# The first token group's output projection, taken from the trunk to the mixer's end

## The chip, the cores and the metric

One of the eight cores of a Trainium2 chip. The metric is the device time of one execution in microseconds (us); before the change the median of three runs is 3453.26 us (3449.13 to 3471.99). TensorE (PE) does the matmuls, VectorE (DVE) and ScalarE (ACT) elementwise work, GpSimd (POOL) some of it and some transfers; SyncE (SP) issues most transfers. Each engine works its instructions off in order.

## The reference

One step of a two-layer decoder for a prompt of 1024 tokens and 64 sample tokens, all in float32. The first layer, as far as it matters here:

```
o_tok = rwkv7_mix(rms_norm(x))              # 768 columns, 12 heads, a scan over the tokens
o_mem = memory_attention(q_mem, k, v)       # 256 columns, 4 heads over 256 memory tokens
x = x + concat([o_tok, o_mem]) @ W_o[l]     # 1024 x 1024
f = conv_glu(rms_norm(x, norm_ffn[l]), ...) # the feed-forward part
x = x + f
```

The keys and values of the memory are made for both layers from the same memory tokens. The second layer is of the same kind with latent attention in place of the scan; the outputs are both token sets after a last norm, and the states.

## The kernel before, in words

Activations lie transposed: 1024 features in eight blocks (KC = 8) of 128 partitions, tokens along the free dimension. Prompt and sample tokens form one row of 1088 columns, worked in three groups G3 of 364, 364 and 360. A float32 operand is split into a high part (an ACT cast) and a low remainder (a subtraction on DVE, or on POOL inside the mixer), and each product is three matmuls: wh xh, wh xl, wl xh (`gemm_y`, L477 to L479). Weights come in raw tiles `wr` of 128 x 512 (three buffers, filled from SP, L207), are cast to `wh` (L210) and leave the remainder `wl` (L211), four buffers each.

**The mixer** (`mixer_a`) works head pairs in two token halves. Several generators are merged by weights: at each step the one that is least far on, for its weight, emits its next instructions. `last` ends the mixer: the inner part and scan of the last pair (`main`), the pair before it (`side`) and as filler the first layer's memory attention (L2111 to L2241), and then the second layer's memory keys and values (`memory_kv`, L2051 to L2096). TW holds the weights: TW[4] filler steps beside the chain, TW[7] beside the last output step `a_out` (L1019 to L1058). The mixer's outputs go to the DRAM tensor `od`, through `y` (L1056).

**The trunk** (`Step.trunk_tail` for the first layer) loads `od` group by group into `xl` from POOL's queue (L1452), splits it (L1458, L1459), and fills the stream `x` from nine row tiles `xt` of two buffers (L1140) by eight PE transposes (L1152) and two ACT copies (L1154) each. Then it multiplies: column blocks d = 0 to 3 for the three groups, then d = 4 to 7, each followed by the residual add (L1162), a square (L1167, L1170) and a sum of squares on POOL (L1171). The norm of one group runs beside the products of the next.

A scheduler orders each engine's instructions by the program's order and its own estimates; an instruction that waits holds up all behind it on its engine. A transfer issued from SP or POOL waits at its issue until its buffer is free.

Of the kernel before, what the change touches and what calls it, by code (L numbers as in the profile page):

```python
# [9 lines left out]
F32 = mybir.dt.float32  # L10
F32R = mybir.dt.float32r
I32 = mybir.dt.int32
BF16 = mybir.dt.bfloat16
AF = mybir.ActivationFunctionType
ALU = mybir.AluOpType
# [4 lines left out]
NP_ = 1024  # L20
NS = 64
NT = NP_ + NS
KC = 8
# [62 lines left out]
G3 = [(0, 364), (364, 364), (728, 360)]  # L86
# [14 lines left out]
class Step:  # L101
# [168 lines left out]
            s.nc.sync.dma_start(out=xt[h], in_=s.I["x_prompt"][0, 128 * i:128 * i + 128, 512 * h:512 * h + 512])  # L270
        return xt

    def mixer_a(s, od, qmd, kvd):
        nc, tc = s.nc, s.tc
        s.wl_eng = nc.gpsimd
        ap = s.ap_
        s.od, s.qmd = od, qmd
        s.gate = {}
        s.TW = (50, 0, 110, 0, 60, 10, 50, 120)
        s.PW = (15, 20, 0, 40, 15, 0)  # L280

        def ld(name, shape):
# [33 lines left out]
        for nme, cnt in (("mu_r", 6), ("mu_k", 6), ("mu_v", 6), ("mu_la", 1), ("mu_g0", 1), ("mu_g1", 1)):  # L316
            o = s.t(ap, [128, cnt], "o" + nme, 1)
# [23 lines left out]
        def last(fill):  # L341

            u0, u1 = units[-2:]
            h, p = u1
            c = ctx[u1]

            def main():

                s.ended = True
                yield from s.a_inner(p, h, c)  # L350
                c["y"] = s.t(ap, [128, 576], "y", 2)
                for g in s.groups(h)[:2]:
                    yield from s.a_chain(p, h, c, *g, ("ab", "tp"))

            def side():
                yield from chain(u0)
                while "y" not in c:
                    yield
                yield from s.a_chain(p, h, c, 8, 1)

            w = s.TW
            yield from s.mergeg([(main(), w[0], w[1]), (side(), w[2], w[3]), (s.take(fill, w[4]), w[4])])
            yield from s.mergeg([(s.a_out(p, h, c), w[5], w[6]), (fill, w[7])])
# [5 lines left out]
        for i in range(nu):  # L369
            g = []  # L370
# [10 lines left out]
                g.append((mkv, 22))  # L381
            s.merge(g)
        s.mslot = (ap, "xn", 584, 16)
        s.drain(last(s.seq(s.mem_attention(0, qmd, kvd, od, ("mm", "sm", "sm")), s.memory_kv(kvd, 1, ("sm", "mm", "mm")))))

    def rot(s, name):
        l = getattr(s, name)
# [748 lines left out]
    def x_tile(s, i, eng):  # L1136

        xt = s.st([128, 1024], "xt", 2)
        src = s.I["x_prompt"][0, 128 * i:128 * i + 128] if i < 8 else s.I["x_sample"].rearrange("b t d -> (b t) d")
        eng.dma_start(out=xt[:128 if i < 8 else 64], in_=src)  # L1140
        return xt

    def load_x(s, first):

        nc, x = s.nc, s.x
        for i in range(9):
            rows = 128 if i < 8 else 64
            xt = first[i] if i < len(first) else s.x_tile(i, nc.sync)
            for h in range(2):
                q = s.pst("tp")  # L1150
                for k in range(4):
                    nc.tensor.transpose(q[:, k * 128:k * 128 + rows], xt[:rows, 512 * h + 128 * k:512 * h + 128 * k + 128], s.ident[:rows, :rows])  # L1152
                qv = q.rearrange("p (k t) -> p k t", t=128)[:, :, :rows]
                nc.scalar.copy(x[:, 4 * h:4 * h + 4, 128 * i:128 * i + rows], qv)  # L1154
            yield

    def residual(s, d, g, p, acc):
# [268 lines left out]
    def trunk_tail(s, l, od, xd, qmd, xst):  # L1426

        nc, I = s.nc, s.I
        with s.phase(f"f{l}", {"mm": 4, "dn": 2, "tp": 2}):
            s.xp = s.sp  # L1430
            s.ntb, s.LAG = 4, 2
            xdv = xd.rearrange("(k p) t -> p k t", p=128)
            xs = []

            def normed(g, acc):
                xs.append(s.new_xg())
                return s.norm_x(g, acc, ("norm_ffn", 8 * l), xs[-1])

            with s.sub(f"o{l}"):
                os_ = []  # L1440
                first = []
                if l == 0:

                    sh = dict(acc=([128, 364], "acc", 2), nt=([128, 364], "nt", 4), wl=([128, 4, 128], "wl", 8, F32R), wh=([128, 4, 128], "wh", 8, F32R), xt=([128, 1024], "xt", 2))
                    s.lay(*[sh[z] for z in ('wl', 'wh', 'acc', 'nt', 'xt')])
                for c0, n in G3:
                    if c0 == G3[1][0] and l == 0:
                        first = [s.x_tile(i, nc.gpsimd) for i in range(2)]
                    xh, xl = (s.t(s.xp, [128, KC, 364], z, 3, F32R) for z in ("xh", "xl"))
                    m = min(n, NP_ - c0)  # L1450
                    f = xl.bitcast(F32)
                    nc.gpsimd.dma_start(out=f[:, :, :m], in_=od[0].rearrange("(k p) t -> p k t", p=128)[:, :, c0:c0 + m])  # L1452
                    if m < n:
                        nc.gpsimd.dma_start(out=f[:, :, m:n], in_=od[1].rearrange("(k p) t -> p k t", p=128))
                    os_.append((xh, xl, n))
                def parts(xh, xl, n):
                    for k in range(KC):
                        nc.scalar.copy(xh[:, k, :n], xl[:, k, :n].bitcast(F32))  # L1458
                        nc.vector.tensor_tensor(xl[:, k, :n], xl[:, k, :n].bitcast(F32), xh[:, k, :n].bitcast(F32), ALU.subtract)  # L1459
                        yield  # L1460

                xs_ = [(g, [(xh[:, k], xl[:, k]) for k in range(KC)], 0) for g, (xh, xl, n) in zip(G3, os_)]
                with s.tc.manual_schedule(engines={mybir.EngineType.Activation, mybir.EngineType.DVE}):
                    ws = [s.load_w([(I["w_o"][l, :, 0:128], 0, 128)])]
                    s.drain(parts(*os_[0]))
                    ws += [s.load_w([(I["w_o"][l, :, 128 * d:128 * d + 128], 0, 128)], ring=(s.sp, 8)) for d in range(1, 4)]
                if l == 0:
                    s.drain(s.load_x(first))
                acc = {c0: s.st([128, 364], "acc", 2) for c0, n in G3[:2]}
                acc[G3[2][0]] = s.last_acc()  # L1470
                for d0 in (0, 4):
                    if d0:
                        ws = [s.load_w([(I["w_o"][l, :, 128 * d:128 * d + 128], 0, 128)], ring=(s.sp, 8)) for d in range(d0, d0 + 4)]
                    pend = s.emit(s.gemm_t(ws, d0, xs_, acc, normed if d0 else None, () if d0 else [parts(*z) for z in os_[1:]]))
            xl = []

            def stored(g, acc):
                c0, n = g
                nc.sync.dma_start(out=xdv[:, :, c0:c0 + n], in_=s.x[:, :, c0:c0 + n])
                xl.append(s.new_xg())  # L1480
                return s.split_x(g, acc, xl[-1])

            with s.sub(f"n{l}"):
                pend = s.emit(s.ffn(l, xs, pend, stored if l == 0 else s.final, s.first_latent if l == 0 else None))
                if l:
                    s.drain(pend)
            if l == 0:
                s.ntb = 3
                with s.sub("lat"):
                    s.latents(xl, qmd, pend, xst)  # L1490
        if l:
            xst.close()
# [799 lines left out]
    def run(s):  # L2292
        nc, tc = s.nc, s.tc
        s.ps = s.psb = s.sp = None
        dp = s.ctx.enter_context(tc.tile_pool(name="dp", bufs=1, space=bass.MemoryType.DRAM))
        dt = lambda shape, n: s.t(dp, shape, n, 1)
        s.dp, s.wsum = dp, {}
        od = dt([1024, NP_], "odp"), dt([1024, NS], "ods")
        xd, kvd = dt([1024, NT], "xd"), dt([2, 2, 128, 512], "kvd")
        qmd = [dt([256, NT], f"qmd{l}") for l in range(2)]  # L2300
        with s.phase("a", {"mm": 2, "sm": 1, "so": 1, "ab": 1, "tp": 1, "ch": 1, "y": 1}):
            s.a_begin()
            s.consts()
            s.consts_b()
            s.mixer_a(od, qmd[0], kvd)
        s.wl_eng = nc.vector
        s.trunk_tail(0, od, xd, qmd[1], s.stream(0, "right"))
        xst = s.attention(qmd[1], kvd, od, xd)
        Seven(s).trunk_tail(1, od, xd, None, xst)


class Seven(Step):
# [22 lines left out]
    def squares(s, h, acc):  # L2335

        nc = s.nc
        for d in range(KC):
            for c0, a in acc.items():
                xv = s.x[:, d, c0:c0 + QT]  # L2340
                if d == 0:
                    nc.scalar.activation(a, xv, AF.Square)
                else:
                    sq = s.st([128, QT], "nt", s.ntb)
                    nc.scalar.activation(sq, xv, AF.Square)
                    nc.gpsimd.tensor_tensor(a, a, sq, ALU.add)
            yield
# [416 lines left out]
```

## Time and profile before

| | |
|---|---|
| median of three runs | 3453.26 us |
| the profiled execution | 3465.75 us, span 3464.0 us |
| PE busy | 3314.6 us, 96% |
| DVE, ACT, POOL busy | 59%, 43%, 18% |
| mean granted clock of PE | 0.966 |
| DMA | 347 MB, mean 100 GB/s |

Times in the rows are us from the span's start. Busy time is summed over one engine's instructions. A value in brackets behind an instruction is how long its engine stood idle before it, and what ended that. Matmuls overlap, so a matmul's own duration is longer than the distance to the next.

### The profile page before, as it was taken

Reading aid. Unit: us, or ns where it says so; the run is one execution under the profiler, and the core shown is the slowest. Engines: PE = TensorE matmul, PEld = TensorE weight load, DVE = VectorE, ACT = ScalarE, POOL = GpSimd, SP = SyncE. Lnnn points to the kernel's source line nnn. Section 1 sums busy time; section 2 is a strip of 40 time slices with the busy share of each in tenths; the row PEclk is TensorE's granted clock in tenths of the full one; section 3 lists DMA queues with packets and bytes.
Section 4 is the critical chain, followed back from the end, with each engine's and each line's share of the span. In section 5 each row is a group of like instructions: output and inputs, shape, how many; then the busy total and the mean of one; then the engine's idle time right before and its main releaser. Section 6 shows DMA issues by size and latency. Waiting matters only on the chain. (4 is left out here: it accounts for less than half of the span.)

```text
span 3464.0 us, 63205 instructions
## 1 busy us (share of the span) xinstructions
PE 3314.6 (96%) x24362; PEld 2844.6 (82%) x24362; DVE 2060.9 (59%) x4790; ACT 1502.6 (43%) x3355; POOL 633.3 (18%) x982
## 2 busy tenths in 40 slices
PE   6999999999979999999999999899999999999998
PEld 5555677776569999999999888655669999989998
DVE  5776666776535433334345477634446777787776
ACT  5555445544544312212125445433344545454444
POOL 4323123330011000000003100111113211132221
PEclk9998699998889999999999999999999999999999
DMA  4212011113151435425334210454332544544443
GB/s 119 59 32 85 22 39 35 45 46 98 31 169 59 133 93 113 124 82 110 115 78 104 83 47 28 146 173 164 133 94 83 173 138 143 146 133 141 136 139 116
DMA packets 452626, 347.01 MB, mean 100 GB/s; under 512 B 46202, under 2 KB 425870, under 8 KB 446948
## 3 DMA queue, kind: packets, MB, share of 16 engines
q1 hardware_dynamic: 434052, 263.31, 25.7%
q0 software_dynamic: 14368, 75.00, 7.7%
q10 hardware_dynamic: 3904, 4.65, 0.4%
q8 instruction: 191, 3.13, 0.4%
q14 instruction: 111, 0.91, 0.1%
HBM read 317.13 MB, written 71.89 MB: 112 GB/s over the span
## 5 line engine op out<-in xcount | busy, mean ns | idle before, releaser
L477 PE MATMUL pmm<-xh,wh 128*128 128x364 f32 (+3 forms) x1544 | 509.0, 330 | 4.4 <-ACT xh L2662 3.3
L479 PE MATMUL pmm<-xh,wl 128*128 128x364 f32 (+3 forms) x1544 | 503.6, 326 | 0.0
L478 PE MATMUL pmm<-xl,wh 128*128 128x364 f32 (+3 forms) x1544 | 503.3, 326 | 0.2
L210 ACT CAST wh<-wr 128x512 fp32r<-128x512 f32 (+3 forms) x381 | 219.6, 584 | 392.2 <-PE pmm L478 200.3
L2478 PE MATMUL pmm<-xh,uh 128*128 128x272 f32 x1232 | 357.1, 290 | 4.7 <-ACT uh L2434 3.2
L2479 PE MATMUL pmm<-xl,uh 128*128 128x272 f32 x1232 | 355.9, 289 | 1.6 <-DVE xl L1134 1.6
L2480 PE MATMUL pmm<-xh,ul 128*128 128x272 f32 x1232 | 356.8, 290 | 0.0
L477 PE MATMUL pdn<-hh,wh 128*128 128x272 f32 (+2 forms) x1080 | 329.4, 305 | 3.6 <-DVE x L2324 1.9
L479 PE MATMUL pdn<-hh,wl 128*128 128x272 f32 (+2 forms) x1080 | 328.5, 305 | 0.8 <-DVE wl L211 0.8
L478 PE MATMUL pdn<-hl,wh 128*128 128x272 f32 (+2 forms) x1080 | 328.3, 305 | 0.3 <-DVE hl L1134 0.3
L211 DVE TENSOR_TENSOR wl<-wr,wh 128x512 fp32r<-128x512 f32 (+3 forms) x289 | 187.0, 652 | 208.8 <-ACT wh L210 206.7
L477 PEld LDWEIGHTS pmm<-xh,wh 128*128 128x128 f32 (+1 forms) x1544 | 290.9, 188 | 9.1 <-ACT xh L2662 3.7
L2434 ACT CAST uh<-wa 128x512 fp32r<-128x512 f32 x305 | 188.5, 620 | 244.2 <-PE pmm L2479 155.5
L478 PEld LDWEIGHTS pmm<-xl,wh 128*128 128x128 f32 (+1 forms) x1544 | 291.2, 189 | 2.7 <-issue 0.5
L479 PEld LDWEIGHTS pmm<-xh,wl 128*128 128x128 f32 (+1 forms) x1544 | 291.5, 189 | 1.0
L2435 DVE TENSOR_TENSOR ul<-wa,uh 128x512 fp32r<-128x512 f32 x305 | 216.4, 715 | 49.6 <-ACT uh L2434 37.4
L2478 PEld LDWEIGHTS pmm<-xh,uh 128*128 128x128 f32 x1232 | 232.8, 189 | 5.9 <-ACT uh L2434 3.6
L2479 PEld LDWEIGHTS pmm<-xl,uh 128*128 128x128 f32 x1232 | 232.9, 189 | 2.2 <-DVE xl L1134 2.2
L2480 PEld LDWEIGHTS pmm<-xh,ul 128*128 128x128 f32 x1232 | 232.6, 189 | 0.2 <-DVE ul L2435 0.2
L477 PE MATMUL pmm<-xn,wh 128*128 128x292 f32 (+2 forms) x552 | 206.7, 374 | 3.7 <-DVE e L507 3.7
L477 PEld LDWEIGHTS pdn<-hh,wh 128*128 128x128 f32 x1080 | 202.8, 188 | 6.0 <-ACT hh L1133 3.5
L479 PEld LDWEIGHTS pdn<-hh,wl 128*128 128x128 f32 x1080 | 202.6, 188 | 1.8 <-DVE wl L211 1.3
(792 smaller groups left out, 7509.9 us busy)
## 6 DMA issues: line engine op xcount, KB each, us to landing
wa<-in_w_ffn_up SPq DMA_DIRECT2D x131, 256.0 KB
wr<-in_w_ffn_down SPq DMA_DIRECT2D x114, 256.0 KB
wr<-in_w_ffn_up SPq DMA_DIRECT2D x89, 256.0 KB
wr<-in_w_in_a SPq DMA_DIRECT2D x84, 256.0 KB
wr<-in_w_o SPq DMA_DIRECT2D x48, 256.0 KB
wa<-ws1vg SPq DMA_DIRECT2D x44, 256.0 KB
wa<-ws1all SPq DMA_DIRECT2D x44, 256.0 KB
wa<-ws1vgg SPq DMA_DIRECT2D x43, 256.0 KB
```

The lines of the kernel that those rows point to most:

```text
L210: nc.scalar.copy(wh[:, :n, :m], wr[:, :n, :m])
L211: s.wl_eng.tensor_tensor(wl[:, :n, :m], wr[:, :n, :m], wh[:, :n, :m].bitcast(F32), ALU.subtract)
L477: nc.tensor.matmul(ps[:m, :n], wh[:, :m], xh[:, c0:c0 + n], start=(k == 0), stop=False)
L478: nc.tensor.matmul(ps[:m, :n], wh[:, :m], xl[:, c0:c0 + n], start=False, stop=False)
L479: nc.tensor.matmul(ps[:m, :n], wl[:, :m], xh[:, c0:c0 + n], start=False, stop=(k == last))
L2434: nc.scalar.copy(wh, w)
L2435: nc.vector.tensor_tensor(wl, w, wh.bitcast(F32), ALU.subtract)
L2478: nc.tensor.matmul(p, wh, xh[:, k], start=k == 0, stop=False)
L2479: nc.tensor.matmul(p, wh, xl[:, k], start=False, stop=False)
L2480: nc.tensor.matmul(p, wl, xh[:, k], start=False, stop=k == 3)
```

## The change

A new generator `early_out` is put behind the memory keys and values in the filler. It reloads the first 364 prompt columns of `od` (eight pieces, from SP), splits them, and for each of eight column blocks loads w_o and the matching columns of x, multiplies, transposes x on PE, adds both, and writes the block to the DRAM tensor `xd`. The trunk then loads `od` and fills `x` for groups 1 and 2 alone, loads group 0 of `x` from `xd`, and squares it in a generator of its own; the products of group 0 leave the trunk. Two weights of TW change.

```diff
-        s.TW = (50, 0, 110, 0, 60, 10, 50, 120)
+        s.TW = (50, 0, 110, 0, 100, 10, 50, 160)
...
-        s.drain(last(s.seq(s.mem_attention(...), s.memory_kv(kvd, 1, ("sm", "mm", "mm")))))
+        s.drain(last(s.seq(s.mem_attention(...), s.memory_kv(kvd, 1, ("sm", "mm", "mm")), s.early_out(od, xd))))
+
+    def early_out(s, od, xd):
+
+        nc, I = s.nc, s.I
+        n = G3[0][1]
+        xs = []
+        for k in range(KC):
+            xh, xl = (s.t(s.ap_, [128, 584], "xn", 16, F32R)[:, :n] for _ in range(2))
+            nc.sync.dma_start(out=xl.bitcast(F32), in_=od[0][128 * k:128 * k + 128, :n])
+            xs.append((xh, xl))
+        for xh, xl in xs:
+            nc.scalar.copy(xh, xl.bitcast(F32))
+            nc.vector.tensor_tensor(xl, xl.bitcast(F32), xh.bitcast(F32), ALU.subtract)
+            yield
+        for d in range(KC):
+            c = slice(128 * d, 128 * d + 128)
+            xr = s.t(s.wp, [128, 4, 128], "wr", 3)
+            nc.sync.dma_start(out=xr[:, :2], in_=I["x_prompt"][0, 0:256, c].rearrange("(i p) f -> p i f", p=128))
+            nc.sync.dma_start(out=xr[:n - 256, 2], in_=I["x_prompt"][0, 256:n, c])
+            w = s.load_w([(I["w_o"][0, :, c], 0, 128)])
+            p = s.pst("mm")
+            for k in range(KC):
+                (wh, wl), (xh, xl) = w[k], xs[k]
+                nc.tensor.matmul(p[:, :n], wh, xh, start=k == 0, stop=False)
+                nc.tensor.matmul(p[:, :n], wh, xl, start=False, stop=False)
+                nc.tensor.matmul(p[:, :n], wl, xh, start=False, stop=k == KC - 1)
+                yield
+            q = s.pst("sm")
+            for i in range(3):
+                r = min(128, n - 128 * i)
+                nc.tensor.transpose(q[:, 128 * i:128 * i + r], xr[:r, i], s.ident[:r, :r])
+            o = s.t(s.ap_, [128, 588], "ext", s.XB)[:, :n]
+            nc.scalar.copy(o, q[:, :n])
+            nc.vector.tensor_tensor(o, o, p[:, :n], ALU.add)
+            nc.sync.dma_start(out=xd[c, :n], in_=o)
+            yield
...
-        for i in range(9):
-            rows = 128 if i < 8 else 64
-            xt = first[i] if i < len(first) else s.x_tile(i, nc.sync)
+        for i in range(6):
+            xt, rows = first[i] if i < len(first) else s.x_tile(i, nc.sync)
+            c0 = G3[0][1] + 128 * i
...
-                for c0, n in G3:
-                    if c0 == G3[1][0] and l == 0:
+                for c0, n in G3[1:]:
+                    if c0 == G3[2][0]:
                         first = [s.x_tile(i, nc.gpsimd) for i in range(2)]
...
+                g0 = G3[0]
+                nc.gpsimd.dma_start(out=s.x[:, :, :g0[1]], in_=xdv[:, :, :g0[1]])
...
+                def squares():
+                    a = acc[0][:, :g0[1]]
+                    for d in range(KC):
+                        xv = s.x[:, d, :g0[1]]
+                        sq = s.st([128, 364], "nt", s.ntb) if d else a
+                        nc.scalar.activation(sq[:, :g0[1]], xv, AF.Square)
+                        if d:
+                            nc.gpsimd.tensor_tensor(a, a, sq[:, :g0[1]], ALU.add)
+                        yield
+
-                xs_ = [... for g, (xh, xl, n) in zip(G3, os_)]
+                xs_ = [... for g, (xh, xl, n) in zip(G3[1:], os_)]
...
-                    pend = s.emit(s.gemm_t(ws, d0, xs_, acc, normed if d0 else None, () if d0 else [parts(*z) for z in os_[1:]]))
+                    pend = s.emit(s.gemm_t(ws, d0, xs_, acc, normed if d0 else None, [normed(g0, acc)] if d0 else [parts(*os_[1]), squares()]))
```

How the change moves instructions is read from the order of each engine's program; a line number there is that of the kernel it stands in. First PE at the mixer's end, before: the second half of the output step (`pso`), then the memory keys and values, whose tokens are transposed (`psm`) and multiplied (`pmm`, 128x512).

```order
L1051 MATMUL pso_11146<-g1s_5988,wh_10698 128x288
L1048 MATMUL pso_11152<-g0h_5872,wh_10698 128x288
L1049 MATMUL pso_11152<-g0l_5873,wh_10698 128x288
L1050 MATMUL pso_11152<-g0h_5872,wl_10699 128x288
L1051 MATMUL pso_11152<-g1s_5988,wh_10698 128x288
L2068 MATMUL psm_10980<-ident_93,xn_10954 128x128
```

And now (`wr` under `psm` is the column block of x that `early_out` transposes):

```order
L1087 MATMUL pso_11570<-g1s_5988,wh_10881 128x288
L415 MATMUL psm_11316<-ident_93,wr_11273 128x128 x2
L2138 MATMUL pmm_11001<-xn_11008,xn_11003 128x512
L2138 MATMUL pmm_11002<-xn_11008,xn_11003 128x512
L415 MATMUL psm_11316<-ident_93,wr_11273 128x108
L2139 MATMUL pmm_11001<-xn_11009,xn_11003 128x512
L2140 MATMUL pmm_11001<-xn_11008,xn_11003 128x512
L2139 MATMUL pmm_11002<-xn_11009,xn_11003 128x512
L2140 MATMUL pmm_11002<-xn_11008,xn_11003 128x512
L1084 MATMUL pso_11576<-g0h_5872,wh_10881 128x288
```

The token transposes and the first of eight weight chunks now stand ahead of the output step's last part; the early block's 192 matmuls follow behind the eighth chunk.

SP's queue in the early block, now: the reload of `od` (L393) behind the memory result's six writes (L2145 to L2148).

```order
L393 DMA xn_11137<-odp_63 128x364
L2145 DMA kvd_66<-xn_11126 128x512
L2147 DMA out_mem_k_p<-xn_11126 128x256
L2148 DMA out_mem_v_p<-xn_11126 128x256
L2145 DMA kvd_66<-xn_11131 128x512
L2147 DMA out_mem_k_p<-xn_11131 128x256
L2148 DMA out_mem_v_p<-xn_11131 128x256
L393 DMA xn_11140<-odp_63 128x364
```

Before, these writes were followed by a tile of x, and nothing reloaded `od` from SP. Further on in SP's queue, the loads of the last column block (`wr`, from in_x_prompt and in_w_o) and the write of the sixth:

```order
L419 DMA xd_65<-ext_11468 128x364
L403 DMA wr_11520<-in_x_prompt 108x128
L207 DMA wr_11523<-in_w_o 128x4x128
L207 DMA wr_11529<-in_w_o 128x4x128
```

The loads of column block 8 stand directly behind the write of column block 6.

POOL at the border between mixer and trunk, before (`xl` is the operand of a group, `xt` a tile of x):

```order
L405 TENSOR_TENSOR rstd_10974<-ms_10971,mhalf_91 128x2
L1452 DMA xl_11181<-odp_63 128x8x364
L1140 DMA xt_11183<-in_x_prompt 128x1024
L1140 DMA xt_11185<-in_x_prompt 128x1024
L1452 DMA xl_11188<-odp_63 128x8x364
```

And now:

```order
L211 TENSOR_TENSOR wl_11526<-wr_11523,wh_11525 128x512
L211 TENSOR_TENSOR wl_11532<-wr_11529,wh_11531 128x512
L1492 DMA xl_11605<-odp_63 128x8x364
L1177 DMA xt_11607<-in_x_prompt 128x1024
L1177 DMA xt_11609<-in_x_prompt 128x1024
L1492 DMA xl_11612<-odp_63 128x8x296
L1494 DMA xl_11612<-ods_64 128x8x64
L1497 DMA x_11589<-xd_65 128x8x364
```

The first load of the trunk stood behind the memory tokens' norm; it now stands behind the last weight remainder of the early block.

## Rows read from the trace of the kernel before

**Rows 1.** The core's span and clock, and from the profile's page the busy time and the busy tenths of PE and its granted clock in 40 slices.

```profile
core 0: 3464.0 us, clock 0.966
PE 3314.6 (96%) x24362; PEld 2844.6 (82%) x24362; DVE 2060.9 (59%) x4790; ACT 1502.6 (43%) x3355; POOL 633.3 (18%) x982
PE   6999999999979999999999999899999999999998
PEclk9998699998889999999999999999999999999999
```

**Rows 2.** Stretches around the mixer's end: length, then busy us (and instructions) of PE, its weight loads, DVE, ACT and POOL, PE's granted clock, the share of the DMA engines, GB/s.

```profile
922.20:946.50 24.30, 23.26 (x227) 15.27 (x226) 15.05 (x56) 13.47 (x50) 0.00 (x0) 1.00 0.12 29
946.50:960.20 13.70, 7.79 (x45) 4.77 (x42) 4.46 (x13) 9.55 (x20) 0.00 (x0) 0.89 0.32 98
960.20:986.20 26.00, 19.58 (x64) 13.69 (x64) 11.40 (x23) 10.95 (x23) 3.66 (x5) 0.66 0.56 191
...
986.00:992.00 6.00, 4.14 (x25) 3.33 (x23) 4.68 (x10) 6.00 (x15) 2.23 (x3) 1.00 0.80 251
992.00:1001.00 9.00, 1.64 (x11) 1.30 (x12) 0.79 (x2) 1.66 (x4) 0.00 (x0) 0.85 1.05 378
1001.00:1020.00 19.00, 18.56 (x115) 17.37 (x116) 11.71 (x22) 16.05 (x36) 1.33 (x1) 0.89 0.66 202
...
1036.00:1100.00 64.00, 64.00 (x386) 63.53 (x385) 25.67 (x43) 25.62 (x44) 15.01 (x15) 1.00 0.24 73
```

**Rows 3.** PE's timeline from the output step to the first memory product: start, duration of the piece, instruction, count, idle time before it and what ended it.

```profile
958.76 0.61 PE L1048 MATMUL pso<-g0h,wh 128*128 128x288 f32 x1 [3.85 <-DVE y L1052]
...
962.41 0.45 PE L2068 MATMUL psm<-ident,xn 128*128 128x128 f32 x1 [2.33 <-DVE xn L408]
...
965.02 1.12 PE L2068 MATMUL psm<-ident,xn 128*128 128x128 f32 x4 [0.68 <-ACT xn L2070]
...
971.32 0.79 PE L2086 MATMUL pmm<-xn,xn 128*128 128x512 f32 x1 [1.59 <-ACT xn L1133]
```

**Rows 4.** The memory keys and values: SP's weight loads, a late cast, and two products that follow each other.

```profile
961.50 19.09 SPq L2081 DMA_DIRECT2D xn<-in_w_mem_kv  x8
...
978.00 0.39 PE L2088 MATMUL pmm<-xn,xn 128*128 128x512 f32 x1
...
978.23 0.39 PE L2087 MATMUL pmm<-xn,xn 128*128 128x512 f32 x1
...
981.51 0.62 ACT L1133 CAST xn<-xn 128x512 fp32r<-128x512 f32 x1 [2.11 <-DMA xn<-in_w_mem_kv]
```

**Rows 5.** PE's waits from 800 to 1030 us, by who was waited for: total, times, longest.

```profile
PE ptp L1152 <- DMA xt<-in_x_prompt: 7.2, 1, 7.2
PE pso L1048 <- DVE y L1052: 4.7, 2, 3.8
...
PE pmm L477 <- ACT xh L1458: 1.1, 1, 1.1
```

**Rows 6.** The first and last of SP's six writes of the memory result, and ACT's eight casts of group 0's operand.

```profile
986.43 0.33 SPq L2093 DMA_DIRECT2D kvd<-xn  x1
...
989.35 0.43 SPq L2096 DMA_DIRECT2D out_mem_v_p<-xn  x1
...
986.78 3.28 ACT L1458 CAST xh<-xl 128x364 fp32r<-128x364 f32 x8
```

**Rows 7.** One weight tile of w_o: its issue on SP, the cast that waited for it, and the weight remainders on POOL over the whole run (min/median/max ns).

```profile
1054.00 0.37 SPq L207 DMA_DIRECT2D wr<-in_w_o  x1
...
1056.56 0.62 ACT L210 CAST wh<-wr 128x512 fp32r<-128x512 f32 x1 [3.31 <-DMA wr<-in_w_o]
...
L211 POOL TENSOR_TENSOR wl<-wr,wh x92: 450/1283/1989, 23.7 to 773.1; 128x512 fp32r<-128x512 f32 x88, 128x128 fp32r<-128x128 f32 x4
```

**Rows 8.** POOL's loads of the three groups' operands: when issued, and the time to landing over them.

```profile
961.70 1.08 POOL L1452 DMA_DIRECT2D xl<-odp  x1
...
985.56 1.79 POOL L1452 DMA_DIRECT2D xl<-odp  x2 [21.52 <-DVE xn L1134]
...
DMA to landing us min/median/max: 8.4/10.1/11.9
```

**Rows 9.** The third tile of x: its issue, PE's transposes that waited for it, matmuls behind that wait, matmuls some us later, and eight transposes without a wait.

```profile
989.95 0.36 SPq L1140 DMA_DIRECT2D xt<-in_x_prompt  x1
...
1001.01 1.94 PE L1152 MATMUL ptp<-ident,xt 128*128 128x128 f32 x8 [7.22 <-DMA xt<-in_x_prompt]
...
1003.66 0.51 PE L477 MATMUL pmm<-xh,wh 128*128 128x364 f32 x1
1003.96 0.51 PE L478 MATMUL pmm<-xl,wh 128*128 128x364 f32 x1
...
1005.14 0.33 PE L479 MATMUL pmm<-xh,wl 128*128 128x364 f32 x1
1005.30 0.33 PE L477 MATMUL pmm<-xh,wh 128*128 128x364 f32 x1
...
1006.97 1.04 PE L1152 MATMUL ptp<-ident,xt 128*128 128x128 f32 x8
```

More of the change, by code (lines that the diff above doesn't have):

```diff
@@ L271, in a_load, with mixer_a @@
         return xt
-    def mixer_a(s, od, qmd, kvd):
+    def mixer_a(s, od, qmd, kvd, xd):
         nc, tc = s.nc, s.tc
@@ L383, in mixer_a @@
         s.mslot = (ap, "xn", 584, 16)
-        s.drain(last(s.seq(s.mem_attention(0, qmd, kvd, od, ("mm", "sm", "sm")), s.memory_kv(kvd, 1, ("sm", "mm", "mm")))))
+        s.drain(last(s.seq(s.mem_attention(0, qmd, kvd, od, ("mm", "sm", "sm")), s.memory_kv(kvd, 1, ("sm", "mm", "mm")), s.early_out(od, xd))))
+    def early_out(s, od, xd):
[32 more added lines that the diff above has]
+            yield
     def rot(s, name):
@@ L1138, in x_tile @@
         xt = s.st([128, 1024], "xt", 2)
-        src = s.I["x_prompt"][0, 128 * i:128 * i + 128] if i < 8 else s.I["x_sample"].rearrange("b t d -> (b t) d")
-        eng.dma_start(out=xt[:128 if i < 8 else 64], in_=src)
-        return xt
+        c0 = G3[0][1] + 128 * i
+        n = min(128, NP_ - c0)
+        eng.dma_start(out=xt[:n], in_=s.I["x_prompt"][0, c0:c0 + n])
+        if n < 128:
+            eng.dma_start(out=xt[n:n + NS], in_=s.I["x_sample"].rearrange("b t d -> (b t) d"))
+            n += NS
+        return xt, n
     def load_x(s, first):
         nc, x = s.nc, s.x
-        for i in range(9):
-            rows = 128 if i < 8 else 64
-            xt = first[i] if i < len(first) else s.x_tile(i, nc.sync)
+        for i in range(6):
+            xt, rows = first[i] if i < len(first) else s.x_tile(i, nc.sync)
+            c0 = G3[0][1] + 128 * i
             for h in range(2):
@@ L1153, in load_x @@
                 qv = q.rearrange("p (k t) -> p k t", t=128)[:, :, :rows]
-                nc.scalar.copy(x[:, 4 * h:4 * h + 4, 128 * i:128 * i + rows], qv)
+                nc.scalar.copy(x[:, 4 * h:4 * h + 4, c0:c0 + rows], qv)
             yield
@@ L1460, in parts @@
                         yield
-                xs_ = [(g, [(xh[:, k], xl[:, k]) for k in range(KC)], 0) for g, (xh, xl, n) in zip(G3, os_)]
+                def squares():
[7 more added lines that the diff above has]
+                        yield
+                xs_ = [(g, [(xh[:, k], xl[:, k]) for k in range(KC)], 0) for g, (xh, xl, n) in zip(G3[1:], os_)]
                 with s.tc.manual_schedule(engines={mybir.EngineType.Activation, mybir.EngineType.DVE}):
@@ L1466, in trunk_tail @@
                     ws += [s.load_w([(I["w_o"][l, :, 128 * d:128 * d + 128], 0, 128)], ring=(s.sp, 8)) for d in range(1, 4)]
-                if l == 0:
-                    s.drain(s.load_x(first))
+                s.drain(s.load_x(first))
                 acc = {c0: s.st([128, 364], "acc", 2) for c0, n in G3[:2]}
@@ L2304, in run @@
             s.consts_b()
-            s.mixer_a(od, qmd[0], kvd)
+            s.mixer_a(od, qmd[0], kvd, xd)
         s.wl_eng = nc.vector
```

## The prediction

> **What bounds the kernel now.** I read the profile's page first: TensorE (PE) is busy 96% of the 3464.0 us span, and the busy tenths show where the rest is: the first slice, and the twelfth (about 953 to 1039 us), with 7 tenths [rows 1]. The kernel is bound by PE, so an edit is worth something only where PE stands still or runs at its lower clock. The change touches only the end of the mixer and the first output projection; from the feed-forward part on, PE's order is the same in both kernels. So the second view is the table by stretches around that place [rows 2]. From 946.5 to 960.2 us, the last head pair's output step, PE works 7.79 of 13.7 us. From 960.2 to 986.2, the second layer's memory keys and values, it works 19.58 of 26.0, at a mean clock of 0.66. From 986 to 1020, group 0 of the projection with the fill of the stream, it works 24.3 of 34. Behind that it is full: 386 matmuls in 64.0 us, 0.166 each. So some 22 us of standing still are to be had (5.9 + 6.4 + 9.7), and a few more of low clock.
>
> The third view, PE's timeline and waits, says what ends each pause. The output step waits 3.85 us for a vector step. The transposes of the memory tokens go back and forth with ScalarE from 962.4, and the first product stands at 971.32 [rows 3]. The products then wait for weights: SP needs 19.09 us for eight loads, a cast waits 2.11 us for one, though two products stand 0.23 us apart when nothing is late [rows 4]. At the fill, the longest wait is 7.2 us for the third tile of x; the first operand of the projection costs only 1.1 us, as its load ran under the memory products [rows 5].
>
> **The change part by part** (+ is slower; the profiled execution is the base).
>
> *The moved product.* 192 matmuls (8 column blocks of 8 x 3) of 364 columns leave the trunk, 192 x 0.166 = 31.8 us, and come in at the mixer's end at the same price: 0. The order shows where: not in the waits of the last chain, but in one block behind the last product of the memory keys and values. No pause of the mixer is filled by it.
>
> *Transposes of x.* 72 before (nine tiles of eight), 48 + 24 now. Eight take 1.04 us [rows 9], 0.13 each. Nine of the 24 now stand among the waits of the output step: -1.2.
>
> *The memory keys and values.* More of the attention is drawn into the chain (the table's 60 becomes 100), so this work starts inside the chain and the output step. The front, 960.2 to 971.3, goes off the path: -11.1. What hides it is the 5.9 us in which PE stood in the output step; if ScalarE, which is busy there, holds it up, half of it stays: bound -6. The products took 971.3 to 986.2, 14.9 us. The first of eight weight chunks is now used before the output step ends, the second is loaded by then; the third is queued on SP behind the write of the output step, and the last ones wait for free tiles. Six loads at 2.6 us landing, two by two, put the end about 13 us after that write: -2. Bounds: -5 (42 products at 0.23 make 9.7 us), 0.
>
> *The reload of the operand.* Before, POOL issued it at 961.70, under the memory products. Now seven of the eight pieces stand on SP behind the six writes of the memory result. Those run from 986.43 to 989.78, 3.35 us; the nearest landing is a weight tile, issued at 1054.00 and cast at 1056.56, 2.56 us; a cast is 3.28 / 8 = 0.41 [rows 6, 7]. PE does the first piece (0.5 us) and waits 3.4 + 2.6 + 0.4 - 0.5 = 5.9 us, less the 1.1 that stood there: +5 (bounds 0 to +9).
>
> *Weights for the early block.* It reads all of w_o once more: 16 loads, 16 casts of 0.62 us, 16 remainders on POOL of 1.28 us. ScalarE and POOL have room (POOL worked 3.66 of the 26.0 us before it [rows 2]), so by themselves they cost nothing. But x, and both weight halves, go through three raw tiles. A weight tile holds its place 2.56 + 0.62 + 1.28 = 4.5 us, and the last columns' loads queue on SP behind the write of the column two before. A column block takes PE 24 x 0.166 + 3 x 0.13 = 4.4 us; with issue the ring needs about 4.8. Five blocks: +2 (bounds 0 to +8).
>
> *The border.* This is the new wait. POOL issues the operand of group 1 behind its last weight remainder, some 1.5 us before the early block ends; behind that load in turn stand two tiles of x, group 2's operand, and the early result coming back from DRAM. Such a load landed in 8.4 to 11.9 us [rows 8]. 8.4 + 0.5 for the first cast and remainder - 1.5 = about 7.5: +7.5. Bounds: +0.4 if POOL is two blocks ahead, +12 for the slow landing. The Trainium skill, page "DMA: Bandwidth & Descriptors", section "Anatomy of one DMA — SWDGE (gpsimd) path", fits 2.0 us plus bytes / 436e3; for 1456 KB that makes an estimate of 5.4 us, and the sum would be 3 us lower by it. The rows show 8.4 at the least, and I go by them.
>
> *The third tile of x.* It still takes the first tile's place, so it is issued after the first eight transposes (989.95), and PE stands for it until 1001.01 [rows 9]. The same loads of about 3 MB are under way beside it, but they start earlier against it: I take 4 us for 7.2: -3 (bounds -7 to +1). The upper bound holds a further wait: ScalarE's squares of group 0 need the early result back, and the last copies of x are queued behind them.
>
> *Clock.* After the 7.2 us pause the matmuls stood 0.30 us apart until about 1005 (the lower level of 1.2 GHz), then 0.166: 4 us at half rate, 2 us lost [rows 9]. One pause becomes two: +2 (bounds 0 to +4).
>
> *The chain's filler.* By the order, 28 rows of the attention move forward, into stretches with waits; then three steps of the chain stand without filler. At 922.2 to 946.5 PE worked 23.26 of 24.3 [rows 2], so what leaves shortens it until the chain's own latency binds. Nothing shows that latency alone: 0 (bounds -4 to +4).
>
> **Sum:** 0 - 1.2 - 11.1 - 2 + 5 + 2 + 7.5 - 3 + 2 + 0 = -0.8 us. The profiled execution took 3465.75 us (span 3464.0), 12.5 above the median of the three runs, 3453.26. Against the median the sum gives 3452.5.
>
> **The rivals.**
> A, slower: the weight ring. If a column's loads wait for the write just before (one block back, not two), each late block costs 4.4 + add, write, load, cast and remainder, about 10 us; five blocks add 27 in place of the 2, and the time is 3477. It decides from 7 us a block on. For it: all go through one in-order SP queue, whose waits for weight tiles are long already. Against it: the order puts the eighth column's loads behind the sixth column's write.
> B, faster: the border hides. If POOL is ahead, and the loads land under the early block, the border costs 0.4, the reload 1 and the third tile is there: -0.8 - 7.1 - 4 - 4 = -16, 3437. For it: DMA is nearly idle behind the fill (share 0.24 from 1036 on [rows 2]). Against it: POOL's place in its queue, and group 2's operand lies in tiles that the block reads to its end.
> C, the change does what its words say: the block fills the mixer's waits. Then the 22 us go: 3431. The order speaks against it.
>
> **Numbers.** Chances: forecast (within 10 us of its sum) 0.62, A 0.15, B 0.2, C 0.03. The likeliest is the forecast: 3452. The single bounds, added as independent, make about 12 us either way; with B below and most of A above, and the median's own scatter (3449.13 to 3471.99), the range is 3434 to 3474. About 1%, 34.5 us, is what a measurement of this kernel can tell from no change; only C with a better chain, or A with a slow border, comes to it: faster 0.03, same 0.94, slower 0.03.
>
> **What would show it.** Right: the first memory product soon after the output step's last vector step; PE still for some 6 us between the last memory product and the second piece of the early block; 4.4 to 5 us a column; a PE wait of 6 to 9 us on group 1's cast, ended by the load of its operand; a wait of 3 to 6 us for x; the stream from the feed-forward part on unchanged. It is wrong if the border's wait is under 2 us or over 14, if the early block takes over 45 us, or if the chain ends more than 5 us sooner or later than before.

## The result, and the profile after

The changed kernel takes **3491.53 us**, median of six runs (3486.57 to 3494.92), against 3453.38 us for the kernel before in the same set of runs: a ratio of 1.0103, 95% interval 1.0079 to 1.0127, so 27 to 44 us slower. The prediction said 3452, range 3434 to 3474, and gave slower by over 1% a chance of 0.03. It was wrong.

The page of the changed kernel, beside [rows 1]: TensorE (PE) has the same number of matmuls and is busy longer, and the hole in its tenths is wider: the slices from 785 to 1133 us show 8, 8, 7 and 8 tenths, where before only the third of them was below 9.

```profile
span 3487.5 us, 63399 instructions
...
PE 3323.2 (95%) x24362; PEld 2849.9 (82%) x24362; DVE 2061.2 (59%) x4790; ACT 1514.2 (43%) x3375; POOL 655.9 (19%) x998
...
PE   7999899998879999999999999899999999999998
...
PEclk9998799998789999999999999999999999999999
```

To compare the two, I cut both traces at four places that exist in both: an output step of the mixer up to which the order of instructions is the same (802.43 us before, 793.26 after), the start of the last pair's output step, where the chain ends, the first product of group 0, and the last sum of squares of the projection (PE's matmul over the squares). The cuts at 880.00 us and those inside the projection only make the stretches shorter; they are not the same place in both. Stretches of before, PE only: length, busy (instructions), granted clock, DMA share, GB/s.

```profile
802.43:880.00 77.57, 69.18 (x664) 0.85 0.27 79
880.00:947.11 67.11, 61.55 (x530) 0.87 0.13 32
947.11:987.34 40.23, 27.27 (x106) 0.75 0.49 158
987.34:1005.20 17.86, 9.73 (x51) 0.81 1.01 347
1005.20:1112.14 106.94, 106.51 (x655) 1.00 0.22 68
sum 309.71, PE 274.24; mean PE 54.85
```

The same cuts in the changed kernel, with the projection in four pieces (two of the early block, the border, the rest):

```profile
793.26:880.00 86.74, 77.62 (x768) 0.80 0.28 79
880.00:948.33 68.33, 58.30 (x458) 0.84 0.15 44
948.33:982.11 33.78, 26.93 (x84) 0.67 0.33 106
982.11:1006.90 24.79, 20.85 (x111) 0.86 0.53 168
1006.90:1036.80 29.90, 22.63 (x98) 0.83 0.47 140
1036.80:1066.00 29.20, 17.75 (x84) 0.77 0.84 290
1066.00:1134.72 68.72, 67.45 (x406) 1.00 0.25 75
sum 341.46, PE 291.54; mean PE 41.65
```

I call the whole stretch S': 309.7 us before, 341.5 after, **+31.8**. It splits into the chain (144.7 to 155.1: +10.4), the output step with the memory keys and values (40.2 to 33.8: -6.4) and the projection (124.8 to 152.6: +27.8). In the projection PE is idle 15.4 us more (23.9 for 8.6) and *busy* 12.4 us more (128.7 for 116.2), with nine transposes fewer. Most of that is the clock: in the changed kernel's projection the granted clock is at its lower level in six stretches, in which PE works 25.6 us, and before in one, with 4.1 us; at half the pace that makes 12.8 us for 2.0, or +10.8. What makes up the rest is not shown. From the last sum of squares to the end both take the same (2351.9 and 2352.8). The front differs by 9.2 us with the same instructions (e9 and e10 below show differences of this kind without any edit), which is why the two profiled executions are only 24.3 us apart and the medians 38.2.

PE's waits from 1000 to 1100 us in the changed kernel (total, times, longest); the reload's wait of 3.8 us lies at 987:

```profile
PE pmm L513 <- ACT xh L1501: 5.7, 1, 5.7
PE ptp L1192 <- DMA xt<-in_x_prompt: 4.9, 2, 3.8
PE pmm L408 <- ACT wh L210: 3.6, 3, 1.5
PE pmm L410 <- POOL wl L211: 3.0, 4, 0.8
PE ptp L1192 <- ACT x L1194: 0.8, 1, 0.8
PE psm L415 <- ACT ext L417: 0.6, 1, 0.6
```

The first is the border (group 1's operand), then the tiles of x, then the waits for weights inside the early block: 3.6 + 3.0 + 0.6 = 7.2. One turn of the weight ring, from SP, ScalarE, GpSimd and PE, with the matmuls behind it:

```profile
1008.25 1.27 POOL L211 TENSOR_TENSOR wl<-wr,wh 128x512 fp32r<-128x512 f32 x1 [3.57 <-ACT wh L210]
...
1009.55 0.37 SPq L207 DMA_DIRECT2D wr<-in_w_o  x1
...
1012.62 0.62 ACT L210 CAST wh<-wr 128x512 fp32r<-128x512 f32 x1 [4.09 <-DMA wr<-in_w_o]
...
1013.32 1.27 POOL L211 TENSOR_TENSOR wl<-wr,wh 128x512 fp32r<-128x512 f32 x1 [3.80 <-ACT wh L210]
...
1014.64 0.48 PE L410 MATMUL pmm<-xn,wl 128*128 128x364 f32 x1 [0.75 <-POOL wl L211]
1014.93 0.51 PE L408 MATMUL pmm<-xn,wh 128*128 128x364 f32 x1
1015.23 0.51 PE L409 MATMUL pmm<-xn,wh 128*128 128x364 f32 x1
```

A tile of w_o is asked for when the remainder before it has freed its place (1009.52), is cast 3.07 us later, and its own remainder ends 5.07 us after the last one did. A column needs two of them. The column of x sits in the third place until the end of its block. And the matmuls that follow stand 0.30 us apart, in place of 0.166 [rows 9]: the lower level, 1.2 GHz, though the wait had been 0.75 us and the one before it 1.47.

### The profile page after: what moved, and what is told of

Its sections match the earlier page's. It is cut to its first block, busy times and chain, and to the rows that moved or that the text cites. A ratio compares the mean times of both kernels' runs of the same rounds, so it can differ in the third digit from the quotient of the medians.

```text
span 3487.5 us, 63399 instructions
## 1 busy us (share of the span) xinstructions
PE 3323.2 (95%) x24362; PEld 2849.9 (82%) x24362; DVE 2061.2 (59%) x4790; ACT 1514.2 (43%) x3375; POOL 655.9 (19%) x998
## 5 line engine op out<-in xcount | busy, mean ns | idle before, releaser
L513 PE MATMUL pmm<-xh,wh 128*128 128x360 f32 (+3 forms) x1480 | 487.1, 329 | 8.9 <-ACT xh L1501 5.7
L514 PE MATMUL pmm<-xl,wh 128*128 128x360 f32 (+3 forms) x1480 | 482.6, 326 | 1.0 <-DVE xl L1170 0.8
L515 PE MATMUL pmm<-xh,wl 128*128 128x360 f32 (+3 forms) x1480 | 481.5, 325 | 0.0
L210 ACT CAST wh<-wr 128x512 fp32r<-128x512 f32 (+3 forms) x397 | 229.4, 585 | 420.4 <-PE pmm L514 193.1
L513 PEld LDWEIGHTS pmm<-xh,wh 128*128 128x128 f32 (+1 forms) x1480 | 278.2, 188 | 13.7 <-ACT xh L1501 6.0
L514 PEld LDWEIGHTS pmm<-xl,wh 128*128 128x128 f32 (+1 forms) x1480 | 278.5, 188 | 4.3 <-DVE xl L1170 1.5
L515 PEld LDWEIGHTS pmm<-xh,wl 128*128 128x128 f32 (+1 forms) x1480 | 278.6, 188 | 1.0
```

The costliest lines, as they stand in the source:

```text
L210: nc.scalar.copy(wh[:, :n, :m], wr[:, :n, :m])
L513: nc.tensor.matmul(ps[:m, :n], wh[:, :m], xh[:, c0:c0 + n], start=(k == 0), stop=False)
L514: nc.tensor.matmul(ps[:m, :n], wh[:, :m], xl[:, c0:c0 + n], start=False, stop=False)
L515: nc.tensor.matmul(ps[:m, :n], wl[:, :m], xh[:, c0:c0 + n], start=False, stop=(k == last))
```

## The experiments

The runs of an experiment are compared with the kernel before in the same set; its median moved between sets (3453 to 3472 us), so ratios are given. One execution of each kernel is profiled, and it can lie off the median of its runs (before 12.4 us above it, e7 12.1 below). In S' and its parts (chain, memory, projection) the profiles say the following. (The expectations of e1 to e8 measure from a later output step, 860.35 us before; the S they speak of is 251.8 us before and 281.8 in the changed kernel.)

| | ratio (95%) | S' | chain | memory | projection |
|---|---|---|---|---|---|
| before | 1 | 309.7 | 144.7 | 40.2 | 124.8 |
| changed | 1.0103 (1.0079 to 1.0127) | 341.5 | 155.1 | 33.8 | 152.6 |
| e1 weights of the merge only | 1.0025 (1.0005 to 1.0046) | 312.1 | 154.8 | 31.3 | 126.1 |
| e2 changed, merge as before | 1.0081 (1.0055 to 1.0108) | 333.6 | 139.4 | 45.9 | 148.2 |
| e3 ring and remainders | 1.0032 (1.0014 to 1.0049) | 318.7 | 152.0 | 36.1 | 130.6 |
| e4 reload first | 1.0071 (1.0047 to 1.0094) | 334.3 | 155.0 | 31.5 | 147.8 |
| e5 ring only | 1.0052 (1.0032 to 1.0071) | 323.2 | 153.6 | 32.3 | 137.3 |
| e6 remainders only | 1.0052 (1.0034 to 1.0071) | 325.1 | 150.0 | 37.5 | 137.6 |
| e7 = e3 + e4 | 1.0036 (1.0020 to 1.0052) | 314.5 | 151.8 | 36.1 | 126.7 |
| e8 = e7, merge as before | 1.0030 (1.0015 to 1.0044) | 315.7 | 144.7 | 43.6 | 127.4 |
| e9 before, again | - | 307.2 | 141.1 | 39.4 | 126.7 |
| e10 before, five tiles of x | 1.0004 (0.9988 to 1.0021) | 307.8 | 143.3 | 40.7 | 123.8 |
| e11 e7 + five tiles | 1.0033 (1.0014 to 1.0052) | 319.4 | 152.0 | 37.9 | 129.5 |
| e12 e10 + late operands | 0.9971 (0.9957 to 0.9985) | 297.4 | 141.1 | 40.6 | 115.7 |

**The two weights (e1, e2).** e1 is the kernel before with one line changed, e2 the changed kernel with it undone:

```diff
-        s.TW = (50, 0, 110, 0, 60, 10, 50, 120)
+        s.TW = (50, 0, 110, 0, 100, 10, 50, 160)
```

> The kernel before with nothing but the two weights of the changed one (60 to 100, 120 to 160). Theory T, the weights lengthen the chain: from the output step of the last pair but one (860.35 us before, 852.94 after) to the chain's end the changed kernel took 95.4 us where the kernel before took 86.8. If the weights do that, this kernel shows 94 to 97 us there too, gets about 6 us of it back because the memory keys and values start earlier, and takes 3453 to 3459 us. Rival R, the early block's loads do it (they enter SP's queue and the raw weight tiles inside the chain): 86 to 88 us there, and 3445 to 3450 us, as only the gain is left.

> The changed kernel with the two weights of the kernel before (60, 120). T: the chain takes 86 to 89 us again, the memory keys and values get longer by about 6 us, the early block stays at 54 to 56 us: 3487 to 3491 us (3491.5 with the change). R: the chain still takes 94 to 97 us and the memory part is longer as well: 3495 to 3499 us.

e1, its PE stretches:

```profile
793.95:880.00 86.05, 76.64 (x739) 0.80 0.29 80
880.00:948.72 68.72, 58.11 (x486) 0.89 0.22 62
948.72:979.97 31.25, 24.04 (x74) 0.70 0.34 112
979.97:1106.04 126.07, 116.44 (x703) 0.97 0.33 107
```

By the measure of the expectation, e1's chain takes 97.4 us (851.32 to 948.72), e2's 86.5 (864.86 to 951.38). So the weights lengthen the chain, and the early block's loads do not: R falls. In the table, six profiles with the old weights show a chain of 139 to 145 us, eight with the new ones 150 to 155. e1 gets 9.0 back in the memory part and is 0.25% slower. In e2, 15.7 us come back in the chain, but the memory part grows by 12.1, twice what T said; its ratio can't be told from the changed kernel's.

**Ring and remainders (e3, e5, e6).** e3 has both edits, e5 the first alone, e6 the second alone:

```diff
+        s.wl_eng = nc.vector
...
-            xr = s.t(s.wp, [128, 4, 128], "wr", 3)
+            xr = s.e_tile()[:, :384].rearrange("p (i f) -> p i f", f=128)
```

> The changed kernel, but the early block's columns of x lie in tiles of their own, no longer in the ring of three raw weight tiles, and its weight remainders are made on VectorE. T: the waits for weights in the early block (7.2 us in eight pieces) go, and with them the stretches at the lower clock behind them (about 7 us): early block 41 to 45 us in place of 54.7, total 3476 to 3481 us. Rival C, the low clock in the block does not come from these waits: only 5 to 7 us go, 3484 to 3487 us. Rival L, the loads themselves are too slow, whatever tile they take: the waits move to the casts of the weights, ended by their loads, and the time stays at 3488 to 3492 us.

> The changed kernel with only the first half of the edit before: the early block's columns of x in tiles of their own; weight remainders stay on GpSimd. From the output step of the last pair but one to the last sum of squares of the projection (S) the changed kernel took 281.8 us, the kernel before 251.8, the kernel with both halves 259.7. Theory T, two separate causes: the ring of three raw tiles makes the waits inside the block, GpSimd's place in its own queue makes the wait at the border. Then here the waits for weights fall from 7.2 to under 2 us, the border's wait stays at 5 to 8 us: S 268 to 272 us, ratio to the kernel before 1.005 to 1.007. Rival, the ring alone: S 259 to 263, no wait at the border.

> The changed kernel with only the second half: weight remainders of the early block on VectorE, x still in the ring of raw tiles. T: the border's wait goes (under 2 us), most of the waits in the block stay (3 to 6 us, as a remainder takes 0.65 in place of 1.28 us): S 269 to 274 us, ratio 1.005 to 1.008. Rival, the remainders are what makes the ring slow: waits in the block under 1.5 us, S 259 to 264.

In e3 the early block runs from 983.38 to 1024.0, 40.6 us in place of 54.7; no wait for weights is left in the list, and behind the reload's wait PE works without a gap:

```profile
983.40:988.90 5.50, 1.06 (x4) 0.75 0.90 289
988.90:1024.00 35.10, 35.10 (x204) 0.94 0.54 163
```

C and L fall: the low clock went with the waits. S' fell by 22.8, more than T said, because the border went too: GpSimd, without the remainders, issued group 1's operand under the memory products, and PE's wait there is 0.9 us.

```profile
965.70 1.05 POOL L1493 DMA_DIRECT2D xl<-odp  x1 [24.86 <-DMA odp<-y]
...
PE pmm L514 <- ACT xh L1502: 0.9, 1, 0.9
```

Alone, e5 takes 18.3 us off S' and e6 16.3 (S: 266.4 and 267.3); together only 22.8. So they are not two separate causes, as T had it. In e5 the weights are never waited for, and GpSimd ends its remainders sooner: it asks for group 1's operand 10.3 us before the block's end (4.2 in the changed kernel), and the border's wait is 3.2 us, not 5 to 8. In e6 the waits for weights are 2.1 us, and the border's 3.2 stay under another name: the operand was asked for at 983.90, but its casts stand on ScalarE behind the cast of a late tile of w_o:

```profile
1047.66 0.62 ACT L210 CAST wh<-wr 128x512 fp32r<-128x512 f32 x1 [2.33 <-DMA wr<-in_w_o]
1048.19 3.27 ACT L1502 CAST xh<-xl 128x364 fp32r<-128x364 f32 x8
```

**The reload (e4), and all three (e7, e8).** In e4 the loads of seven pieces are emitted before the memory result's writes:

```diff
+        os_ = []
         for i in range(2):
-            o = s.mt([128, 512])
-            nc.scalar.copy(o, ps[i])
+            os_.append(s.mt([128, 512]))
+            nc.scalar.copy(os_[i], ps[i])
+        if l:
+            s.reload()
+        for i in range(2):
+            o = os_[i]
             nc.sync.dma_start(out=kvd[l, i], in_=o)
```

> The changed kernel, but seven of the eight pieces of the reload stand on SP ahead of the six writes of the memory result. T: the wait of 3.8 us behind the first piece becomes 0.5 to 1.5 us, the stretch at the lower clock behind it gets shorter: 3485 to 3489 us. Rival: the pieces wait for their tiles, not for the writes ahead of them on SP; the wait stays above 3 us and the time within 1 us of 3491.5.

> The changed kernel with x in tiles of its own, remainders on VectorE and the reload ahead of the writes. T, the three add: S 251 to 256 us (259.7 less the 4 to 7 us of the reload's run), no longer than the kernel before: ratio 1.000 to 1.003. Rival, the load of weights for the memory keys and values or the tiles of x take up what is gained: S 258 to 262, ratio 1.003 to 1.005.

> As the run before, with the two weights of the kernel before. T: chain 86 to 89 us in place of 95, the memory keys and values 6 us longer: S 249 to 255, ratio 0.998 to 1.002. Rival, the longer memory part costs more than the chain gives: S 257 or more, ratio above 1.003.

e4's longest wait for a piece is 1.2 us, S' falls by 7.2: T, though its ratio can't be told from the changed kernel's. e7's S' is 4.8 above before, and in the list of its waits the early block has 2.0 us for the pieces and 0.9 at the border, nothing else; its clock there is full:

```profile
944.32:980.39 36.07, 24.29 (x83) 0.84 0.58 197
980.39:1020.00 39.61, 37.32 (x224) 1.00 0.54 169
1020.00:1107.09 87.09, 79.90 (x473) 0.96 0.38 123
```

The profile says T (S 255.9), the runs say 1.0036, which is the rival's range (7 to 18 us). The profiled execution was a fast one, so the two need not contradict each other, but what lies between them stays open. Part of the rival's mechanism is in the profile. Behind the output step the memory products take 19.4 to 19.7 us in e3, e6 and e7, where GpSimd asks for group 1's operand and two tiles of x ahead of the block, and 14.9 to 15.2 in the changed kernel, e4 and e5; in e7 their casts wait for late weights, at a DMA share of 0.85 in place of 0.47.

```profile
959.63:979.30 19.67, 12.91 (x42) 0.91 0.85 291
...
972.89 0.62 ACT L1180 CAST xn<-xn 128x512 fp32r<-128x512 f32 x1 [3.75 <-DMA xn<-in_w_mem_kv]
```

So what the border gains is in part paid there, which may also be why e5 and e6 do not add; no run takes the two apart. e8 (S 257.7, 1.0030) fits the rival: what its chain gives (144.7) its memory part takes (43.6). Either way, with every wait of the early block mended, the projection takes 126.7 and 127.4 us, against 124.8 and 126.7 before. In the projection the early block then costs nothing, and it gains nothing.

**How much the untouched part moves (e9).**

> The kernel before, unchanged, for a second profile of it: how far the part that no edit touches moves from execution to execution. Theory V: the mixer's clock moves it; from the output step at 730.15 us to the next at 758.53 (28.4 us in the profile of before, 24.2 in four of the others, 29.9 in two) the same instructions take 24 to 30 us, and from the output step at 802.43 to the last sum of squares (S', 309.7 us) it is 303 to 310. Rival: the part does not vary beyond 1 us, and the differences there are the kernels' own.

The same two output steps of the same kernel, in the profile of before and in e9's, as stretches:

```profile
730.15:758.53 28.38, 28.04 (x361) 0.82 0.13 31
```

```profile
733.87:758.07 24.20, 23.84 (x362) 1.00 0.15 36
```

V holds: 4.2 us on a stretch of 28, at a granted clock of 0.82 or 1.00, with no edit. The front moves too: the output step that stood at 802.43 us before stands at 802.52 in e9 and at 794.04 in e10, whose mixer is that of before. S' is 307.2, but the chain alone takes 139.4 to 144.7 us in the six profiles with the old weights, so differences of S' under about 5 us mean nothing here.

**The fill, in the kernel before (e10, e12) and in e7 (e11).** e10 raises the tiles of x from two to five and loads all five ahead of the operands of groups 1 and 2; e11 does that to e7, and has the early result back ahead of group 2's operand; e12 is e10 with those two operands loaded from SP behind the seventh and ninth tile, and with SP's loads of x kept in the order of the program (the diff is cut to the main lines):

```diff
-        xt = s.st([128, 1024], "xt", 2)
+        xt = s.st([128, 1024], "xt", 5)
...
-                        first = [s.x_tile(i, nc.gpsimd) for i in range(2)]
+                        first = [s.x_tile(i, nc.gpsimd) for i in range(5)]
...
+            if i in (6, 8):
+                s.late[(6, 8).index(i)]()
```

> The kernel before with five tiles of x in place of two, all five loaded from GpSimd ahead of the operands of groups 1 and 2. T: the 7.2 us in which TensorE waited for the third tile fall under 1.5 us and the stretch at the lower clock behind them (about 2 us) goes: S' 300 to 303 us, ratio 0.997 to 0.999. Rival: the operands of groups 1 and 2, now later, make the wait in its place: ratio 0.999 to 1.002.

> The early projection with x in tiles of its own, remainders on VectorE and the reload first (S' 314.5 us, ratio 1.0036), and now five tiles of x and the early result's return ahead of group 2's operand. T: of the 5.4 us of waits at the fill under 2 are left: S' 308 to 312 us, ratio 1.001 to 1.003. Rival, ScalarE holds the copies of x up because its cast waits for the early result's last write: the 4.4 us stay, ratio 1.003 to 1.005.

> The kernel before with five tiles of x (as two runs ago, where the wait for the third tile only became a wait of ScalarE for a tile of w_o), and now the operands of groups 1 and 2 loaded from SP behind the seventh and the ninth tile of x, so that they no longer share the DMA engines with x and w_o at the fill. T, the bytes asked for at once make the wait: of 7 to 8 us of waits at the fill under 3 are left, S' 301 to 304 us (309.7 and 307.2 in two profiles of before), ratio 0.997 to 0.999. Rival, TensorE then waits for the operand of group 1, as at the border of the changed kernel: a wait of 3 us or more on its cast, S' 306 or more, ratio 0.999 to 1.002.

e10: T falls. The wait for a tile of x is gone, but PE now stands 6.15 us for ScalarE, which stands at the cast of a late tile of w_o with the copies of x behind it.

```profile
993.50 0.90 PE L1152 MATMUL ptp<-ident,xt 128*128 128x128 f32 x3 [6.15 <-ACT x L1154]
...
992.34 0.62 ACT L210 CAST wh<-wr 128x512 fp32r<-128x512 f32 x1 [6.37 <-DMA wr<-in_w_o]
```

e11 has the rival's ratio and its wait, 7.5 us for ScalarE's copies, but not its reason: as in e10, ScalarE stands at the cast of a late tile of w_o (7.71 us). e12 keeps the five tiles and moves only the loads that nobody needs yet. The waits of its projection are:

```profile
PE pmm L477 <- ACT xh L1466: 1.1, 1, 1.1
PE ptp L1152 <- ACT x L1154: 0.8, 1, 0.8
PE ptp L1152 <- ACT xh L1466: 0.4, 1, 0.4
```

T: S' is 297.4 (below the 301 to 304 expected; the projection gives 9.1 to 11.0 us of it, and 3.6 or 0 are the chain, which no edit touched), the ratio 0.9971. **This is faster than both kernels**, 0.15 to 0.43% under before, without the early block. The DMA engines stay nearly as full as in e10 (share 0.93 between 981.5 and 1000 us, where PE's clock is 1.00; 1.04 in e10 from 978 to 996): what helped is, as far as these runs tell, which loads they are asked for first. That the two loads also moved from GpSimd's queue to SP's was not tested by itself, nor was the late place with two tiles of x.

## Why the prediction was wrong, step by step

- **What bounds the kernel** held: PE's order and the tail are unchanged, and every loss lies between the mixer's last head pairs and the last sum of squares. That the product comes in one block, and fills no wait of the mixer, held too (rival C out).
- **Clock, +2 (0 to +4): this is the step that failed most.** The projection has 12.4 us more of busy time, 13.6 with the 1.2 of the nine transposes, and 10.8 of it are time at the lower level. I read the price off one pause of 7.2 us [rows 9] and argued that one pause becomes two. There were a dozen waits more, and six stretches at the lower level in place of one. Three of them (15.3 us of PE's work) stand behind the long waits of 3.8, 5.7 and 3.8 us, one more than I had counted here, though all three stand in my own sum as waits. The other three, 10.2 us together, stand among the short waits for weights (0.55 to 1.47 us; 1014.9 to 1017.7 above is one), which I had priced at their own length alone. e3 and e7 show it the other way round: where the waits go, the granted clock of the block is 0.94 and 1.00.
- **The chain's filler, 0 (-4 to +4): it measured +10.4**, and e1 puts +10.1 of it on the two weights alone. The stretches below run from the output step of the last pair but one to a step of the scan that stands in both kernels, and from there to the chain's end; before first, then changed.

```profile
860.35:922.20 61.85, 54.98 (x531) 0.83 0.13 35
922.20:947.11 24.91, 23.41 (x228) 1.00 0.12 28
...
852.94:927.02 74.08, 66.63 (x621) 0.84 0.13 35
927.02:948.33 21.31, 16.23 (x163) 0.80 0.28 75
```

  The late stretch, which I had looked at [rows 2], got 3.6 us shorter, inside my bound, for 7.2 us of work that left it. The one ahead of it got 12.2 us longer for 11.7 us of work that came in: its 6.9 us of standing still were not filled. (The last 1.8 us lie ahead of both.) I had said that the filler moves into stretches with waits, and gave its arrival no price.
- **The memory keys and values, -11.1 - 2 = -13.1: it measured -6.4.** The front went, as said: the first product stands at 961.97, ahead of the output step's last part. But it was not hidden: the output step took 17.5 us (948.33 to 965.87) for 13.0 before (947.11 to 960.09), at a granted clock of 0.60 for 0.89, so the front is worth -6.7, near the bound of -6. And the products behind it took 15.2 us for 14.9, not 13. In e1, without the early block, they took 13.1 (the output step 17.0): SP asks for the last five weight tiles from 969.57 on, behind the early block's x and w_o, and in e1 from 967.22. The output step, before and then changed:

```profile
947.11:960.09 12.98, 7.64 (x41) 0.89 0.34 104
...
948.33:965.87 17.54, 13.41 (x42) 0.60 0.23 72
```

- **The reload, +5: 3.8.** Mechanism and place as said (e4: 1.2 with the loads ahead of the writes).
- **The weight ring, +2 (0 to +8): 7.2**, inside its bounds. I had 4.5 us per place and three places; but one of the three holds x for a whole column, and a turn took 5.07. Rival A was right that the ring is the trouble and wrong on what makes it: from 990 to 1037 us the loads of w_o stood on SP 15.9 us for GpSimd's remainders, and the writes ahead of them only 1.7 us.
- **The border, +7.5: 5.7**, with the releaser as said. The load was asked for 4.2 us before the block's end, not 1.5, and landed in 9.5 us, not 8.4; group 2's took 14.4. The Trainium skill's fit in "DMA: Bandwidth & Descriptors", section "Anatomy of one DMA — SWDGE (gpsimd) path", gives an estimate of 5.4 us for this size; no load of this size here came near it, the DMA engines' share being 0.96 over these 9.5 us and 0.97 over the 8.4 us before. Rival B needed GpSimd ahead of the block; e3 made it so, and the wait was 0.9.
- **The third tile of x, -3: -2.6** (5.7 us of waits at the fill for 8.3; the third tile costs 1.1 of them, the fourth 3.8).

So the waits were put right to within 3 us together (+14.1 for +11.5), in part by luck, as the ring was 5.2 us too low and the reload and the border 3.0 too high. The sum failed on what was not a wait: 11.6 us of busy time (13.6 for 2), 10.4 of chain, and 6.7 too much credit for the memory part. Together these are 28.7 of the 32.6 us between -0.8 and +31.8. Two of the tests that the prediction named told it: the early block took 54.7 us (wrong over 45), and the chain got longer by more than 5; its end at 948.33, only 1.2 later than before, hid that, since the front had come 9.2 us sooner.

## What to carry to other kernels

On an engine that is nearly always busy, count pauses, not only their sum: here 7.2 us of short waits for weights came with 10.2 us of matmuls at half the pace, 5.1 us more. A merge weight that pulls filler into a chain that is nearly full (55.0 of 61.9 us) lengthens the chain by about the work that comes in, while what leaves gave back half of its own, so price both. And before a product is moved to fill a hole, look whether the hole is a matter of order: with five tiles of x, putting the operands of groups 1 and 2 behind them took the wait away, and 0.29% of the time, where the moved product cost 1%.

## What the hardware showed that was not expected

- The same 28 us of the mixer took 28.4 or 24.2 us in two executions of one kernel, at a granted clock of 0.82 or 1.00. Two profiles, one of each kernel, can differ by this without any edit.
- The length of a wait did not tell what it cost in clock. After the 5.74 us pause at the border, matmuls stood 0.30 us apart from 1045.6 until 1048.8, then 0.166; after the waits of 1.47 and 0.75 us before 1014.9, 0.30 as well; after those of 1.11 and 0.75 us before 1009.9, 0.166 at once.
- A transfer of 1456 KB landed in 8.4 us at best before and in 9.5 in the changed kernel, with the DMA engines' share at 0.97 and 0.96 meanwhile; one of 1184 KB right behind it took 14.4. The Trainium skill, page "Trainium Kernel Development and Optimization", section "Key Constraints", says that transfers from all queues run on the same 16 engines and that issuing from several only saves issue time. e10 and e12 fit that and do not test it by itself: between them the two loads changed both queue and place, and a wait of 6.15 us went, with none over 1.1 left.
